# A decoder trunk on one core: turning the gate tokens of the recurrent layer by transposing transfers

## The chip, the core and the metric

The kernel runs on one core of a Trainium2 chip. The metric is the device time of one execution in microseconds; comparisons are made between medians of several runs. The profile is of one execution. Engines: TensorE (PE, with its weight loads as PEld), VectorE (DVE), ScalarE (ACT), GpSimd (POOL) and SyncE (SP), which issues nearly all transfers.

## The reference

256 tokens of width 1024 pass through two layers. Each layer is a SwiGLU FFN, a token mixer and a second FFN, with norms around each. The mixer of the first layer is the recurrent block that the change touches; that of the second is attention over a shared K/V.

```python
def recurrent_block(x, w_in, conv_w, conv_b, w_a, b_a, w_x, b_x, lam, w_out):
    gx = x @ w_in                                    # 1024 -> 2 x 1344
    gate, rec = gx[..., :D_RNN], gx[..., D_RNN:]
    rec = causal_depthwise_conv(rec, conv_w, conv_b) # 4 taps
    rec = rg_lru(rec, w_a, b_a, w_x, b_x, lam)       # two block-diagonal gates, then a scan over time
    return (jax.nn.gelu(gate) * rec) @ w_out         # 1344 -> 1024
```

In `rg_lru` the gates r and i are sigmoids, a = exp(-8 r softplus(-lam)), the scan's input is sqrt(1 - a^2) * i * x. All in float32.

## The kernel before

**Arithmetic.** Every float32 product is made of three matmuls of a rounded upper part and the rest: each weight unit (a 512 KB load, `raw`) is split into `whi` (a copy on ACT, L173) and `wlo` (a subtraction on DVE, L177). There are 5 buffers of `raw` and 9 of each part, so loads and splits run ahead of PE. The tokens are two halves of 128 (t = 0, 1).

**The recurrent stage.** The gate half of `w_in` is computed token-major (tokens in the partitions): column groups g = 0, 1, 2 of `GCOLS`, in units `g0` to `g10`. The recurrent half is computed channel-major (channels in the partitions), since convolution and scan run over time: 11 tiles of 126 channels (the last has 84), two to a pair p = 0 to 5, in units `r0a` to `r5a` (`r4b` is the second half of pair 4's weights). `conv` evacuates a pair to `xc` (ACT) and adds three taps from PSUM (DVE); `gw_unit` makes the two gates (PE, into the two `gt` banks), ACT takes their tanh to `th`. `after_gates` makes tanh and exp on ACT and a few DVE steps. When two pairs are through, `batch(g)` is queued for the four tiles of group g: `roots` (Sqrt on ACT over `tt`, and a Gelu on every gate tile collected in `plain`), `u_of`, `scan`, then the gate tokens are turned to channel-major by PE (`gate_T`, into a `tr` bank), and `product` multiplies them with the scan. Its result is split into an upper part (ACT) and a lower one (`low`, DVE), in `yy[g]`, and `row_items` multiplies these with `w_out` (units w0 to w10, one for each tile of 126 channels k).

**The gate tokens.** When a group is complete, its columns are copied from PSUM to a tile of all 1344 columns for its token half:

```python
tok = toks[t][:, c0:c0 + nn]
if (g, t) == (0, 0):
    nc.scalar.activation(tok, ps, AF.Gelu_apprx_tanh)
else:
    nc.scalar.activation(tok, ps, AF.Copy)
    plain.append(tok)
```

Gelu is therefore done in token order, ahead of the turn. On ACT Gelu, exp (with tanh) and Sqrt each need a table of their own; where the function changes, an `ACT_TABLE_LOAD` stands in its list.

**What sets the order.** PE's order is written by hand: `RG_ORDER` (a unit with its token half in front, as `1g7`) and `OUT_ORDER`, which takes the output rows as eight of half 0 (k = 0 to 7), six of half 1, the last three of half 0, the last five of half 1. After each step `tick` counts down deferred work (`defer(n, fn)`) and takes from `queue` as much as a purse allows. The instructions of the other engines come out of these calls and are then put in order by a scheduler by its own estimates, except those in `keep_in_program_order`. Each engine's list is fixed when the program is built and runs in order: an instruction that waits holds all behind it.

**A turn by transfers, as the FFNs have it.** In the FFNs the hidden activations are turned without PE: POOL separates the 16-bit halves of each float32 into two planes (L515), SP issues a transposing transfer of 16-bit elements (L523), POOL joins the halves again (L528).

Of the kernel before, what the change touches and what calls it, by code (L numbers as in the profile page):

```python
# [43 lines left out]
def trunk_kernel(ctx: ExitStack, tc: tile.TileContext, A: dict, out: bass.AP):  # L44
# [13 lines left out]
    def nm(s):  # L58
        uid[0] += 1
        return f"{s}_{uid[0]}"  # L60
# [146 lines left out]
    def new_ss():  # L207
        return spool.tile([P, 2], F32, tag="ss", name=nm("ss"))

# [432 lines left out]
    GCOLS = [(0, 512), (512, 512), (1024, DRNN - 1024)]  # L642
# [6 lines left out]
    toks = {}  # L649
    plain = []  # L650
    xcs, tt, th, yy = {}, {}, {}, {}

    def add_gate_unit(g, k0, kn):
        c0, nn = GCOLS[g]

        def prep():
            return split(load_raw(w_in(c0, nn, k0, kn), P, kn * nn), P, kn * nn)

        def work(t, u):
            if k0 == 0:  # L660
                gacc[(g, t)] = mmbank()
            ps = gacc[(g, t)][:, :nn]
            for j in range(kn):
                k = k0 + j
                mm3(ps, *main_x(t, k), u.hi[:, j * nn:(j + 1) * nn], u.lo[:, j * nn:(j + 1) * nn], k == 0, k == 7)
            if k0 + kn == 8:

                if t not in toks:
                    toks[t] = pools["r"].tile([P, DRNN], F32, name=f"tok{t}")
                tok = toks[t][:, c0:c0 + nn]  # L670
                if (g, t) == (0, 0):
                    nc.scalar.activation(tok, ps, AF.Gelu_apprx_tanh)
                else:
                    nc.scalar.activation(tok, ps, AF.Copy)
                    plain.append(tok)
        rg[f"g{sum(n[0] == 'g' and n[1] != 'w' for n in rg)}"] = len(items)
        items.append((prep, work))

# [138 lines left out]
    def batch(g):  # L817

        pairs = [p for p in (2 * g, 2 * g + 1)]
        tps, ys = {}, {}  # L820

        def roots():
# [3 lines left out]
            while plain:  # L826
                v = plain.pop(0)
                tc.keep_in_program_order(nc.scalar.activation(v, v, AF.Gelu_apprx_tanh))
# [12 lines left out]
        def gate_T(t):  # L841
            tok = toks[t][:, 4 * g * RT:]
            tp = tps[t] = trbank()
            for j in range(len(pairs) * 2 if g < 2 else 3):
                w = width(4 * g + j)
                nc.tensor.transpose(tp[:w, j * P:(j + 1) * P], tok[:, j * RT:j * RT + w], ident)

        def product(t):
# [4 lines left out]
            for (a, b, w) in parts_of(g):  # L853
                tp = tps[t][:w, a * P:b * P].rearrange("p (a b) -> p a b", a=b - a)
                nc.vector.tensor_tensor(y[:w, a:b, :], tp, tt[g][:w, a:b, t * P:(t + 1) * P], ALU.mult)
# [13 lines left out]
        q.append((0.0, key, lambda: (gate_T(0), gate_T(1))))  # L869
# [591 lines left out]
```

## Time and profile before

| | us |
|---|---|
| median of 3 runs | 968.38 (968.07 to 968.71) |
| the profiled execution, its own time | 968.35 |
| its span in the profile | 966.60 |
| span: PE busy | 958.6 |
| span: DVE busy | 640.1 |
| span: ACT busy | 526.1 |
| span: POOL busy | 193.4 |
| recurrent stage (units g0 to the last output row) | about 189.5 to 300.5 |

The busy shares tell which engine is full on average. A view by stretches gives the same for any piece of the span, with the granted TensorE clock (1.00 throughout) and the share of the transfer engines. The timeline gives start, duration and, in brackets, the idle time ahead of an instruction and what ended it. Matmuls are pipelined, so their durations overlap: their cost is the distance of their starts.

### The profile page before, as it was taken

What the parts mean: (1) busy time and instruction counts of PE and PEld (TensorE: products, weight loads), DVE (VectorE), ACT (ScalarE), POOL (GpSimd) and SP (SyncE); (2) the same over time, 40 slices, a digit from 0 to 9 for tenths busy, and PEclk for the clock granted to TensorE, in tenths of its full rate; (3) what the DMA queues carried; (4) which work ended last, traced back from release to release, by engine and by line L of the source; (5) the groups of instructions that cost most, each with busy time, mean ns of one, the idle gap of its engine ahead of it and who ended that gap; (6) DMA issues with size and microseconds to landing.
All of it is one profiled execution on the core that took longest, in us unless ns stands there. A gap on an engine that the chain in (4) does not pass through costs nothing.

```text
span 966.6 us, 13061 instructions
## 1 busy us (share of the span) xinstructions
PE 958.6 (99%) x4687; PEld 798.1 (83%) x4687; DVE 640.1 (66%) x849; ACT 526.1 (54%) x749; POOL 193.4 (20%) x206
## 2 busy tenths in 40 slices
PE   9999999999999999999999999999999999999997
PEld 6888888898888888888899888888887788888885
DVE  6758764668997666664687466665487876666642
ACT  7446543568886554444555345444366855444431
POOL 2722230100001323230112122224120012232200
PEclk9999999999999999999999999999999999999999
DMA  8778986565346787785589679878762468777731
GB/s 286 224 245 235 270 276 194 159 196 161 113 118 224 215 233 206 207 244 192 131 174 325 179 216 260 226 189 288 230 252 77 132 198 236 207 222 236 217 109 44
DMA packets 142646, 196.83 MB, mean 204 GB/s; under 512 B 58798, under 2 KB 81686, under 8 KB 142454
## 3 DMA queue, kind: packets, MB, share of 16 engines
q1 hardware_dynamic: 139782, 188.96, 66.4%
q0 software_dynamic: 2192, 6.51, 2.6%
q8 instruction: 37, 0.61, 0.3%
q10 hardware_dynamic: 608, 0.53, 0.2%
q14 instruction: 27, 0.22, 0.1%
HBM read 182.32 MB, written 3.16 MB: 192 GB/s over the span
## 4 chain that ended last, share of the span: by engine, by line
PE 96%; DVE 1%; issue 1%; ACT 1%; POOLq 0%; POOL 0%; DVEq 0%; ACTq 0%
PE mm L416 16%; PE mm L417 15%; PE mm L420 15%; PE mm L183 13%; PE mm L185 13%; PE mm L184 13%; PE mm L1027 2%; PE gt L767 2%; PE mm L1296 1%; PE mm L190 1%; PE mm L191 1%; PE mm L192 1%; PE gt L214 1%; PE tr L127 0%; ACT pe L1172 0%
## 5 line engine op out<-in xcount | busy, mean ns | idle before, releaser
L177 DVE TENSOR_TENSOR wlo<-raw,whi 128x1024 fp32r<-128x1024 f32 (+5 forms) x329 | 416.4, 1272 | 226.1 <-ACT whi L173 224.8
L173 ACT ACTIVATE whi<-raw 128x1024 fp32r<-128x1024 f32 (+5 forms) x329 | 341.6, 1045 | 315.5 <-PE mm L420 113.2
L416 PE MATMUL mm<-whi,xhi 128*128 128x512 f32 x656 | 256.7, 391 | 0.0
L417 PE MATMUL mm<-wlo,xhi 128*128 128x512 f32 x656 | 255.5, 390 | 0.0
L420 PE MATMUL mm<-whi,xlo 128*128 128x512 f32 x656 | 202.2, 389 | 0.0
L420 PEld LDWEIGHTS mm<-whi,xlo 128*128 128x128 f32 x656 | 123.1, 188 | 26.0 <-DVE xlo L228 0.2
L416 PEld LDWEIGHTS mm<-whi,xhi 128*128 128x128 f32 x656 | 123.2, 188 | 25.7 <-issue 0.7
L417 PEld LDWEIGHTS mm<-wlo,xhi 128*128 128x128 f32 x656 | 123.2, 188 | 25.1 <-DVE wlo L177 0.3
L183 PE MATMUL mm<-whi,hhi 128*128 128x512 f32 x352 | 137.2, 390 | 0.0
L185 PE MATMUL mm<-whi,hlo 128*128 128x512 f32 x352 | 137.0, 389 | 0.0
L184 PE MATMUL mm<-wlo,hhi 128*128 128x512 f32 x352 | 136.9, 389 | 0.0
L528 POOL COPY pl<-prod 128x1024 uint16<-128x1024 uint16 (+1 forms) x48 | 69.6, 1449 | 173.3 <-DMA prod<-pl 173.3
L515 POOL COPY pl<-prod 128x1024 uint16<-128x1024 uint16 (+1 forms) x48 | 64.1, 1335 | 175.8 <-DVE prod L512 107.0
L184 PEld LDWEIGHTS mm<-wlo,hhi 128*128 128x128 f32 x352 | 66.1, 188 | 13.7
L185 PEld LDWEIGHTS mm<-whi,hlo 128*128 128x128 f32 x352 | 66.1, 188 | 13.7
L183 PEld LDWEIGHTS mm<-whi,hhi 128*128 128x128 f32 x352 | 66.1, 188 | 13.5
L198 POOL TENSOR_SCALAR nv<-ss 128x1 f32<-128x1 f32 x22 | 9.6, 438 | 314.1 <-ACT junk L205 314.1
L512 DVE SCALAR_TENSOR_TENSOR prod<-mm,rstd,sil 128x512 f32<-128x512 f32 (+1 forms) x48 | 33.7, 703 | 28.8 <-PE mm L420 23.1
L503 ACT ACTIVATE sil<-mm,rstd 128x512 f32<-128x512 f32 (+1 forms) x48 | 31.1, 650 | 32.9 <-PE mm L420 25.0
L534 DVE TENSOR_TENSOR hlo<-pl,hhi 128x512 fp32r<-128x512 f32 (+1 forms) x48 | 40.1, 835 | 5.1 <-ACT hhi L533 5.1
L183 PE MATMUL mm<-whi,xhi 128*128 128x512 f32 (+1 forms) x112 | 42.8, 382 | 0.0
L185 PE MATMUL mm<-whi,xlo 128*128 128x512 f32 (+1 forms) x112 | 42.5, 379 | 0.0
(217 smaller groups left out, 1075.1 us busy)
## 6 DMA issues: line engine op xcount, KB each, us to landing
raw<-in_ffn_w_down_dram SPq DMA_DIRECT2D x88, 512.0 KB
raw<-in_ffn_w_up_dram SPq DMA_DIRECT2D x80, 512.0 KB
raw<-in_ffn_w_gate_dram SPq DMA_DIRECT2D x78, 512.0 KB
raw<-in_rg_w_in_dram SPq DMA_DIRECT2D x10, 504.0 KB
raw<-in_rg_w_out_dram SPq DMA_DIRECT2D x10, 504.0 KB
raw<-in_ffn_w_gate_dram SPq DMA_DIRECT2D x19, 256.0 KB
raw<-in_ffn_w_up_dram SPq DMA_DIRECT2D x16, 256.0 KB
raw<-in_rg_w_in_dram SPq DMA_DIRECT2D x8, 512.0 KB
```

The costliest lines, as they stand in the source:

```text
L173: up = nc.scalar.activation(hi[:parts, c:c + m], rawv[:, c:c + m], AF.Copy)
L177: nc.vector.tensor_tensor(lo[:parts, c:c + m], rawv[:, c:c + m], hi[:parts, c:c + m].bitcast(F32), ALU.subtract)
L183: nc.tensor.matmul(ps, xh, wh, start=first, stop=False)
L184: nc.tensor.matmul(ps, xh, wl, start=False, stop=False)
L185: nc.tensor.matmul(ps, xl, wh, start=False, stop=last)
L416: nc.tensor.matmul(ps, get_x(t, k)[0], u.hi[:, c], start=k == 0, stop=False)
L417: nc.tensor.matmul(ps, get_x(t, k)[0], u.lo[:, c], start=False, stop=False)
L420: nc.tensor.matmul(ps, get_x(t, k)[1], u.hi[:, c], start=False, stop=k == nk - 1)
L512: nc.vector.scalar_tensor_tensor(pr[:, :nn], ps, rs[t][:, 0:1], s, ALU.mult, ALU.mult)
L515: nc.gpsimd.tensor_copy(halves.rearrange("p (h f) -> p h f", h=2), pr[:, :nn].bitcast(U16).rearrange("p (f h) -> p h f", h=2))
L528: nc.gpsimd.tensor_copy(halves.rearrange("p (f h) -> p h f", h=2), turned.rearrange("p (h a) b -> p h (a b)", h=2))
L534: keep(nc.vector.tensor_tensor(lv, x, hv.bitcast(F32), ALU.subtract))
```

## The change

The column groups become 504, 504 and 336 wide, which is 4, 4 and 2 tiles of 126 and the one of 84, so a group's columns are those of one `batch`. A unit's weights keep a distance of 512 in their buffers where two k are loaded; `split3` splits them through strided views. Each group's tokens get a tile of their own (`tok`, 512 wide, two buffers). `gate_T` is now called when a group is complete: POOL clears the padding and separates the tokens into planes in which each tile of 126 (or 84) columns takes 128, SP issues one transposing transfer back into `tok`, POOL joins the halves to `tokT` (channels in the partitions, tokens along the free axis). The PE transposes and their `tr` banks go. Gelu is done behind the turn, on `tokT`, by a step `gelu` in the queue of `batch`, in program order; `roots` does only Sqrt. `product` reads `tokT` from SBUF instead of PSUM.

```diff
--- before.py
+++ after.py
@@ -206,6 +206,18 @@
 
     def new_ss():
         return spool.tile([P, 2], F32, tag="ss", name=nm("ss"))
+
+    def planes(dst, src):
+
+        nc.gpsimd.tensor_copy(dst.rearrange("p (h f) -> p h f", h=2), src.bitcast(U16).rearrange("p (f h) -> p h f", h=2))
+
+    def swap(turned, halves):
+
+        tc.keep_in_program_order(nc.sync.dma_start(turned.rearrange("p (a b) -> p a b", b=P), halves, transpose=True))
+
+    def join(dst, turned):
+
+        nc.gpsimd.tensor_copy(dst, turned.rearrange("p (h f) -> p h f", h=2))
 
     def to_tp(src, n):
 
@@ -639,42 +651,71 @@
     n_ffn1 = len(items)
 
 
-    GCOLS = [(0, 512), (512, 512), (1024, DRNN - 1024)]
+    GCOLS = [(0, 504), (504, 504), (1008, DRNN - 1008)]
     rg = {}
 
     def w_in(c0, n, k0, kn):
         return A["rg_w_in"][0, k0 * P:(k0 + kn) * P, c0:c0 + n].rearrange("(k p) n -> p k n", p=P)
 
     gacc = {}
-    toks = {}
-    plain = []
+    tokT = {}
     xcs, tt, th, yy = {}, {}, {}, {}
 
     def add_gate_unit(g, k0, kn):
         c0, nn = GCOLS[g]
 
+        step = 1024 // kn // 64 * 64 if kn < 3 else nn
+
         def prep():
-            return split(load_raw(w_in(c0, nn, k0, kn), P, kn * nn), P, kn * nn)
+            raw = new_raw()
+            v = raw[:, :kn * step].rearrange("p (k n) -> p k n", k=kn)
+            nc.sync.dma_start(v[:, :, :nn], w_in(c0, nn, k0, kn))
+            return split3(raw, kn, step, nn)
 
         def work(t, u):
             if k0 == 0:
                 gacc[(g, t)] = mmbank()
             ps = gacc[(g, t)][:, :nn]
             for j in range(kn):
-                k = k0 + j
-                mm3(ps, *main_x(t, k), u.hi[:, j * nn:(j + 1) * nn], u.lo[:, j * nn:(j + 1) * nn], k == 0, k == 7)
+                k, o = k0 + j, j * step
+                mm3(ps, *main_x(t, k), u.hi[:, o:o + nn], u.lo[:, o:o + nn], k == 0, k == 7)
             if k0 + kn == 8:
-
-                if t not in toks:
-                    toks[t] = pools["r"].tile([P, DRNN], F32, name=f"tok{t}")
-                tok = toks[t][:, c0:c0 + nn]
-                if (g, t) == (0, 0):
-                    nc.scalar.activation(tok, ps, AF.Gelu_apprx_tanh)
-                else:
-                    nc.scalar.activation(tok, ps, AF.Copy)
-                    plain.append(tok)
+                tok = pools["r"].tile([P, 512], F32, tag="tok", name=nm("tok"), bufs=2)
+                nc.scalar.activation(tok[:, :nn], ps, AF.Copy)
+                defer(5 if (g, t) == (0, 0) else 0, lambda: gate_T(g, t, tok, nn))
         rg[f"g{sum(n[0] == 'g' and n[1] != 'w' for n in rg)}"] = len(items)
         items.append((prep, work))
+
+    def split3(raw, kn, step, nn):
+
+        if step == nn:
+            return split(raw[:, :kn * nn], P, kn * nn)
+        u = Unit()
+        hi = wpool.tile([P, 1024], F32R, tag="whi", name=nm("whi"), bufs=WB)
+        lo = wpool.tile([P, 1024], F32R, tag="wlo", name=nm("wlo"), bufs=WB)
+        v, hv, lv = (x[:, :kn * step].rearrange("p (k n) -> p k n", k=kn)[:, :, :nn] for x in (raw, hi, lo))
+        nc.scalar.activation(hv, v, AF.Copy)
+        nc.vector.tensor_tensor(lv, v, hv.bitcast(F32), ALU.subtract)
+        u.hi, u.lo = hi, lo
+        return u
+
+    def gate_T(g, t, tok, nn):
+
+        m = 4 if g < 2 else 3
+        halves = hpool.tile([P, 512], F32, tag="t1", name=nm("pl"), bufs=2).bitcast(U16)[:, :2 * m * P]
+        hv = halves.rearrange("p (h j f) -> p h j f", h=2, j=m)
+        src = tok[:, :nn].bitcast(U16)
+        n = nn // RT
+        nc.gpsimd.memset(hv[:, :, :n, RT:], 0)
+        nc.gpsimd.tensor_copy(hv[:, :, :n, :RT], src[:, :2 * n * RT].rearrange("p (j f h) -> p h j f", h=2, f=RT))
+        if n < m:
+            nc.gpsimd.memset(hv[:, :, n, BLK:], 0)
+            nc.gpsimd.tensor_copy(hv[:, :, n, :BLK], src[:, 2 * n * RT:].rearrange("p (f h) -> p h f", h=2))
+        turned = tok.bitcast(U16)[:, :2 * m * P]
+        out = tokT[g, t] = pools["r"].tile([P, 4, P], F32, tag="tokT", name=nm("tokT"), bufs=6)
+        defer(1, lambda: swap(turned, halves))
+        defer(5, lambda: join(out[:, :m, :].rearrange("p a b -> p (a b)").bitcast(U16).rearrange(
+            "p (f h) -> p h f", h=2), turned))
 
     def tiles_of(p):
         return [2 * p, 2 * p + 1] if p < 5 else [10]
@@ -817,15 +858,12 @@
     def batch(g):
 
         pairs = [p for p in (2 * g, 2 * g + 1)]
-        tps, ys = {}, {}
+        ys = {}
 
         def roots():
             for (a, b, w) in parts_of(g):
                 v = tt[g][:w, a:b, :]
                 nc.scalar.activation(v, v, AF.Sqrt)
-            while plain:
-                v = plain.pop(0)
-                tc.keep_in_program_order(nc.scalar.activation(v, v, AF.Gelu_apprx_tanh))
 
         def u_of(p):
             w, m = pw(p), len(tiles_of(p))
@@ -838,12 +876,11 @@
             v = tt[g][:w, 2 * (p % 2) + j, :]
             nc.vector.tensor_tensor_scan(v, th[p][0][:w, j, :], v, 0.0, ALU.mult, ALU.add)
 
-        def gate_T(t):
-            tok = toks[t][:, 4 * g * RT:]
-            tp = tps[t] = trbank()
-            for j in range(len(pairs) * 2 if g < 2 else 3):
-                w = width(4 * g + j)
-                nc.tensor.transpose(tp[:w, j * P:(j + 1) * P], tok[:, j * RT:j * RT + w], ident)
+        def gelu():
+            for t in range(2):
+                for (a, b, w) in parts_of(g):
+                    v = tokT[g, t][:w, a:b, :]
+                    tc.keep_in_program_order(nc.scalar.activation(v, v, AF.Gelu_apprx_tanh))
 
         def product(t):
             y = ys[t] = pools["r"].tile([RT, 4, P], F32, tag="y", name=nm("y"), bufs=2)
@@ -851,8 +888,7 @@
                 yy[g] = [rw.tile([P, 1024], F32R, tag="gy", name=nm("y"), bufs=6).rearrange("p (t a b) -> p t a b", t=2, a=4)
                          for _ in range(2)]
             for (a, b, w) in parts_of(g):
-                tp = tps[t][:w, a * P:b * P].rearrange("p (a b) -> p a b", a=b - a)
-                nc.vector.tensor_tensor(y[:w, a:b, :], tp, tt[g][:w, a:b, t * P:(t + 1) * P], ALU.mult)
+                nc.vector.tensor_tensor(y[:w, a:b, :], tokT[g, t][:w, a:b, :], tt[g][:w, a:b, t * P:(t + 1) * P], ALU.mult)
                 nc.scalar.activation(yy[g][0][:w, t, a:b, :], y[:w, a:b, :], AF.Copy)
 
         def low(t):
@@ -866,7 +902,7 @@
             s = len(tiles_of(p)) / 2
             q.append((1.3 * s, key, lambda p=p: u_of(p)))
             q += [(0.72, key, lambda p=p, j=j: scan(p, j)) for j in range(len(tiles_of(p)))]
-        q.append((0.0, key, lambda: (gate_T(0), gate_T(1))))
+        q.insert(-1, (0.0, key, gelu))
         for t in range(2):
             q.append((0.7, key, lambda t=t: product(t)))
         for t in range(2):
```

In the order of ACT's list, from pair 2's `xc` to the Sqrt of group 0 (`tt`); before:

```order
L720 ACTIVATE xc_2133<-mm_2084,par 126x256 x2
L781 ACTIVATE th_2152<-gt_2139,hb 126x256
L781 ACTIVATE th_2153<-gt_2139,hb 126x256
L781 ACTIVATE th_2152<-gt_2140,hb 126x256
L781 ACTIVATE th_2153<-gt_2140,hb 126x256
L800 ACTIVATE tt_2061<-th_2152,sp_101 126x256 x2
L800 ACTIVATE th_2152<-th_2152,sp_102 126x256 x2
L173 ACTIVATE whi_2335<-raw_2333 128x1008
L173 ACTIVATE whi_2384<-raw_2382 128x672
L825 ACT_TABLE_LOAD
L825 ACTIVATE tt_2061<-tt_2061 126x1024
```

Now:

```order
L761 ACTIVATE xc_2151<-mm_2102,par 126x256 x2
L883 ACT_TABLE_LOAD
L883 ACTIVATE tokT_1893<-tokT_1893 126x512
L822 ACTIVATE th_2171<-gt_2158,hb 126x256
L822 ACTIVATE th_2171<-gt_2159,hb 126x256
L822 ACTIVATE th_2172<-gt_2158,hb 126x256
L822 ACTIVATE th_2172<-gt_2159,hb 126x256
L841 ACTIVATE tt_2078<-th_2171,sp_101 126x256 x2
L841 ACT_TABLE_LOAD
L841 ACTIVATE th_2171<-th_2171,sp_102 126x256 x2
L883 ACT_TABLE_LOAD
L883 ACTIVATE tokT_2071<-tokT_2071 126x512
```

Two Gelu on `tokT`, each with its table load, and a reload of the table of exp stand ahead of the Sqrt (which follows the last row here, with a load of its own); the two splits `whi_2335` and `whi_2384` (r4b and r5a) have gone behind it.

DVE's list around the first reader of that Sqrt. `wlo_2336` and `wlo_2385` before, `wlo_2368` and `wlo_2409` now are the lower splits of r4b and r5a; before:

```order
L805 TENSOR_SCALAR th_2152<-th_2152 126x512
L806 SCALAR_TENSOR_TENSOR th_2153<-tt_2061,th_2152 126x512
L177 TENSOR_TENSOR wlo_2336<-raw_2333,whi_2335 128x1008
L809 SCALAR_TENSOR_TENSOR th_2153<-th_2153,th_2152 126x512
L177 TENSOR_TENSOR wlo_2385<-raw_2382,whi_2384 128x672
L810 TENSOR_SCALAR th_2152<-th_2153 126x512
L833 SCALAR_TENSOR_TENSOR tt_2061<-th_2042,tt_2061 126x512
L833 SCALAR_TENSOR_TENSOR tt_2061<-th_2153,tt_2061 126x512
L834 TENSOR_TENSOR tt_2061<-tt_2061,xc_1952 126x512
L834 TENSOR_TENSOR tt_2061<-tt_2061,xc_2022 126x512
```

Now, from eight rows behind the reader on:

```order
L767 SCALAR_TENSOR_TENSOR xc_2263<-mm_2210,par,xc_2263 126x255
L872 TENSOR_TENSOR tt_2078<-tt_2078,xc_2035 126x512
L767 SCALAR_TENSOR_TENSOR xc_2263<-mm_2210,par,xc_2263 126x254
L877 SCALAR_TENSOR_TENSOR tt_2078<-th_2171,tt_2078 126x256
L767 SCALAR_TENSOR_TENSOR xc_2263<-mm_2210,par,xc_2263 126x253
L877 SCALAR_TENSOR_TENSOR tt_2078<-th_2171,tt_2078 126x256
L177 TENSOR_TENSOR wlo_2368<-raw_2365,whi_2367 128x1008
L891 TENSOR_TENSOR y_2371<-tokT_1893,tt_2078 126x512
L891 TENSOR_TENSOR y_2390<-tokT_2071,tt_2078 126x512
L177 TENSOR_TENSOR wlo_2409<-raw_2406,whi_2408 128x672
L897 TENSOR_TENSOR y_2373<-y_2371,y_2372 126x512
L177 TENSOR_TENSOR wlo_2430<-raw_2427,whi_2429 126x1024
```

The two lower splits stood ahead of L833 (L871 now); they now stand among the products and the low parts of group 0. The reader, L871 on `tt_2078`, stands eight rows above the first row here.

SP's list, with the loads of `w_in`'s last unit and of w0 to w4:

```order
L161 DMA raw_2365<-in_rg_w_in_dram 128x4x252
L216 DMA_TRANSPOSE tok_2066<-pl_2068 128x8x128
L161 DMA raw_2406<-in_rg_w_in_dram 128x8x84
L164 DMA raw_2427<-in_rg_w_out_dram 126x1024
L164 DMA raw_2455<-in_rg_w_out_dram 126x1024
L164 DMA raw_2511<-in_rg_w_out_dram 126x1024
L216 DMA_TRANSPOSE tok_2294<-pl_2296 128x8x128
L164 DMA raw_2532<-in_rg_w_out_dram 126x1024
L216 DMA_TRANSPOSE tok_2348<-pl_2350 128x6x128
L164 DMA raw_2586<-in_rg_w_out_dram 126x1024
```

The three transposing transfers, of (0, 1), (1, 1) and (2, 0), are new; the loads around them stand in the same sequence as before, and none stood between them.

## The prediction

> **What bounds the kernel now.** I read the busy shares and the chain that ended last first, then the stretches of the recurrent stage one by one.
>
> ```profile
> PE 958.6 (99%) x4687; PEld 798.1 (83%) x4687; DVE 640.1 (66%) x849; ACT 526.1 (54%) x749; POOL 193.4 (20%) x206
> PE 96%; DVE 1%; issue 1%; ACT 1%; POOLq 0%; POOL 0%; DVEq 0%; ACTq 0%
> 220.00:240.00 20.00, 20.00 (x138) 18.08 (x138) 16.94 (x30) 18.37 (x29) 0.00 (x0) 1.00 0.59 165
> 240.00:260.00 20.00, 20.00 (x144) 17.99 (x143) 19.53 (x34) 17.61 (x33) 0.00 (x0) 1.00 0.45 142
> 260.00:280.00 20.00, 19.54 (x102) 16.22 (x102) 19.06 (x36) 19.88 (x32) 0.00 (x0) 1.00 0.21 60
> 238.78:288.46 49.68, 49.22 (x293) 42.44 (x293) 48.27 (x84) 44.51 (x72) 0.00 (x0) 1.00 0.40 121
> ```
>
> The last four rows are stretches: limits, length, then busy time of PE, PEld, DVE, ACT and POOL. Over the kernel PE is the bound, and any TensorE instruction taken off is time. In the second half of the recurrent stage two more engines are as full: DVE is busy 48.27 of 49.68 us, ACT 19.88 of 20. Whether DVE is on the path is seen at the last output rows:
>
> ```profile
> L185 PEld LDWEIGHTS mm<-whi,y 126*128 126x128 f32 x40 | 7.5, 188 | 1.7 <-DVE y L861 0.2
> 288.75 0.39 PE L184 MATMUL mm<-wlo,y 126*128 126x512 f32 x1
> 288.98 0.44 PE L185 MATMUL mm<-whi,y 126*128 126x512 f32 x1
> 288.46 0.61 DVE L861 TENSOR_TENSOR y<-y,y 126x256 fp32r<-126x256 f32 x2
> ```
>
> PE reaches the first row of group 2 (k = 8, token half 0) just as DVE has written the low part of its product: the weight load of `y` waits 0.2 us for L861, and the matmul at 288.98 is a little long (0.44 instead of 0.39). PE and DVE arrive together. So the saving on PE counts only if DVE's list also gets shorter by then, and every microsecond by which it gets longer counts in full.
>
> **What is removed.** The PE transposes of the gate tokens, in the chain of waits:
>
> ```profile
> 247.69 0.87 PE tr L846 x8
> 266.49 0.87 PE tr L846 x8
> 267.37 0.46 issue
> 281.18 0.66 PE tr L846 x6
> ```
>
> 0.87 + 0.87 + 0.66 = 2.40 us, and the 0.46 us gap behind the second (PE waits there for a PSUM bank that ACT reads) could go too: at most 2.86. The new widths are neutral. Matmuls of 512 columns start 0.23 us apart (288.75 and 288.98 above), those of 320 columns 0.15:
>
> ```profile
> 244.30 0.31 PE L185 MATMUL mm<-whi,xlo 128*128 128x320 f32 x1
> 244.45 0.31 PE L183 MATMUL mm<-whi,xhi 128*128 128x320 f32 x1
> ```
>
> Both are about 0.45 ns a column, and the columns stay the same: 96 matmuls lose 8 each, 48 gain 16 each. Sum 0.
>
> **ACT, ahead of the square root of group 0.** Before, ACT took the tanh and exp of pair 1, two weight splits (r4b, r5a), then Sqrt. Now it also loads the Gelu table and does one Gelu ahead of those tanh, reloads the exp table, and loads Gelu's again for a second Gelu; the two splits go behind the Sqrt.
>
> ```profile
> 229.30 1.00 ACT L720 ACTIVATE xc<-mm,par 126x256 f32<-126x256 f32 x2
> 231.25 1.57 ACT L781 ACTIVATE th<-gt,hb 126x256 f32<-126x256 f32 x4 [0.95 <-PE gt L767]
> 233.69 1.10 ACT L800 ACTIVATE th<-th,sp 126x256 f32<-126x256 f32 x2
> 234.67 1.71 ACT L173 ACTIVATE whi<-raw 128x1008 fp32r<-128x1008 f32 x2
> 236.39 1.28 ACT L825 ACT_TABLE_LOAD   x1
> 237.69 1.06 ACT L825 ACTIVATE tt<-tt 126x1024 f32<-126x1024 f32 x1
> 240.06 1.15 ACT L828 ACTIVATE tok<-tok 128x512 f32<-128x512 f32 x2
> ```
>
> From these starts: load 1.30, Gelu 0.55, tanh with the step behind them 2.44 (231.25 to 233.69), exp 0.98. From 230.30, when `xc` is done: 230.30 + 1.30 + 0.55 + 2.44 + 1.30 + 0.98 + 1.30 + 0.55 + 1.30 = 240.02 for the start of Sqrt, where it was 237.69. PE has those gates ready at 231.25, so of the first load and Gelu 0.95 us lies in a gap. Sqrt comes **2.3 us later** and ends at 241.08. (The Gelu on the very first copy and its table load go; ACT waits for PE right behind them, so 0.)
>
> **DVE, which waits for that Sqrt.**
>
> ```profile
> 235.89 1.20 DVE L177 TENSOR_TENSOR wlo<-raw,whi 128x1008 fp32r<-128x1008 f32 x1
> 237.00 0.69 DVE L809 SCALAR_TENSOR_TENSOR th<-th,th 126x512 f32<-126x512 f32 x1
> 237.61 0.85 DVE L177 TENSOR_TENSOR wlo<-raw,whi 128x672 fp32r<-128x672 f32 x1
> 238.38 0.42 DVE L810 TENSOR_SCALAR th<-th 126x512 f32<-126x512 f32 x1
> 238.78 1.29 DVE L833 SCALAR_TENSOR_TENSOR tt<-th,tt 126x512 f32<-126x512 f32 x2
> ```
>
> L833 at 238.78 is the first reader of Sqrt. Before, DVE filled the wait with the lower splits of r4b and r5a (235.89 to 237.00 and 237.61 to 238.38, 1.88 us). Now these stand behind the scans of group 0, so DVE waits with nothing to do until 241.08 and then has them on top. From there to the low part of group 2 its list is the same as before: 48.27 us of work, so 241.08 + 48.27 + 1.88 = 291.23 instead of 288.46, if the old 1.41 us of gaps (49.68 - 48.27) close; with them 292.6. **Term A: +2.77 us**, up to 4.18. The product now reads two SBUF operands instead of PSUM and SBUF; same size, I take 0. PE's 2.86 us are swallowed: it only comes earlier to the same wait.
>
> **POOL, which did nothing here.** Its copies lock DVE out:
>
> ```profile
> 75.33 1.90 POOL L515 COPY pl<-prod 128x1024 uint16<-128x1024 uint16 x1 [7.50 <-ACT hhi L533]
> 75.11 1.22 DVE L177 TENSOR_TENSOR wlo<-raw,whi 128x1024 fp32r<-128x1024 f32 x1
> 76.24 1.53 DVE L534 TENSOR_TENSOR hlo<-pl,hhi 128x512 fp32r<-128x512 f32 x1
> 65.61 0.68 DVE L534 TENSOR_TENSOR hlo<-pl,hhi 128x512 fp32r<-128x512 f32 x1
> L534 DVE TENSOR_TENSOR hlo<-pl,hhi 128x512 fp32r<-128x512 f32 x40 | 36.7, 918 | 2.6 <-ACT hhi L533 2.6
> L177 DVE TENSOR_TENSOR wlo<-raw,whi 128x1024 fp32r<-128x1024 f32 x292 | 376.7, 1297 | 217.6 <-ACT whi L173 216.5 <-DMA raw<-in_ffn_w_up_dram 0.4
> 62.20 1.04 POOL L515 COPY pl<-prod 128x1024 uint16<-128x1024 uint16 x1 [3.84 <-DVE prod L512]
> 66.48 1.34 POOL L528 COPY pl<-prod 128x1024 uint16<-128x1024 uint16 x1 [3.24 <-DMA prod<-pl]
> 131.12 0.61 POOL L515 COPY pl<-prod 128x512 uint16<-128x512 uint16 x1
> 134.36 0.78 POOL L528 COPY pl<-prod 128x512 uint16<-128x512 uint16 x1 [2.63 <-DMA prod<-pl]
> ```
>
> The POOL copy that starts at 75.33 sits out DVE's 75.11 instruction (1.90 instead of 1.04), and then DVE's next one sits out the copy (1.53 instead of 0.68, +0.85). Averaged over the FFNs' 96 copies the loss is smaller: 292 x (1.297 - 1.22) + 40 x (0.918 - 0.68) = 32 us, 0.33 each, since DVE has gaps there. Behind 241 us there are eight copies: two planes and a join for each of the last three tiles, less one. By size: 1.02 + 2 x (0.61 + 0.32) + 1.34 + 2 x 1.06 = 6.34 us (0.32 and 1.06 drawn between the rows). Bounds for DVE: 8 x 0.33 = 2.6 and 6.3. DVE is 97% busy here, which speaks for the row at 76.24, but the convolution taps read PSUM, and L512, which does too, shows no such loss. I take the middle, **term B: +4.5 us**. The Trainium skill, "SBUF — State Buffer", section "SBUF: two separate sides", says that a DVE instruction with two SBUF inputs and a GpSimd one that reads SBUF hold one port pair for a whole instruction and the loser blocks; the trace agrees at 76.24. By that rule the product, now with two SBUF inputs, joins those that can be blocked, and the sum would go to the upper bound, 977.5. The copies and joins of the first three tiles meet DVE ahead of its wait for Sqrt and cost 0.
>
> **New waits in the queues.** A transpose on SP waits for POOL's planes copy, with weight loads behind it:
>
> ```profile
> 63.27 1.25 SPq L523 DMA_TRANSPOSE prod<-pl  x1
> 237.12 1.69 SPq L164 DMA_DIRECT2D raw<-in_rg_w_out_dram  x2
> ```
>
> From planes done (63.24) to join (66.48) is 3.24 us, all in 6 to 7. The fourth transpose waits for tokens that ACT copies behind Sqrt, `xc`, two splits, a load and four tanh: 241.08 + 1.00 + 1.71 + 1.30 + 1.57 = 246.7. With 0.6 for that copy, 1.02 for the planes and 1.25 for the issue, w3's load goes out at about 249.6 instead of 237.12. PE wants w3 some 5 us behind the gap at 267.37 (three rows of six matmuls at 0.23 us, 4.1, and the gates): 20 us of cover. ACT comes to its split at about 253.6, behind the product of group 0 (15 DVE instructions from 241.08, some 9 us), two y copies, an exp and two splits: 4 us for the load to land, against 3.24 for the transfer above. I take 0; without that cover ACT would stand in front of `xc` of pair 4. The Gelu waits on ACT are for joins done 5 us or more earlier: 0.
>
> **Sum.** The profiled execution took 968.35 us (span 966.60 plus 1.75); the median of the runs is 968.38. 968.35 + 2.77 + 4.5 = **975.6**. After the stage the program is the same and PE-bound, so nothing is given back. Its own range: 968.35 + 2.77 = 971.1 without any lock, 968.35 + 4.18 + 6.34 = 978.9 with all.
>
> **Rivals.**
> - *Faster (0.14):* the low part of group 2 is not what PE waits for, because the scheduler's shuffle lets DVE come to it no later than before; then PE's saving is plain: 968.35 - 2.86 = 965.5. For it: the wait at L861 is 0.2 us in one place and PE is busy 99%. Against: DVE's list is in order, 97% full, and starts 2.3 us late. It decides if low(t0) of group 2 ends before 288.5.
> - *No change (0.10):* POOL's copies fall on taps and scans, and ACT is up to 1.5 us quicker than my walk: 968.4 to 970.3.
> - *SP stops ACT (0.07):* w3 or w4 lands 3 us later than I think, ACT stands in front of `xc` of pair 4, the taps and gates of pair 4 follow: 975.6 + 3 = 978.6.
> - *A table switch costs twice what its row shows (0.03):* each of the three loads added ahead of Sqrt empties the engine for as long again, 3 x 1.30 = 3.9 more: 979.5. Against: between 236.39 and 237.69 there is room for the load alone. The Trainium skill states such a rule, "ScalarE: Activation LUTs", section "What ACT_TABLE_LOAD costs": some 1380 ns of drain beside 1283 ns of load; by it the estimate would be 3 x 1.38 = 4.1 more.
> - That the transposes stay on PE is out: they are gone from its list.
>
> **Chances.** My forecast has 0.66. Within 0.2% (1.94 us, about what a measurement of this kernel can tell from no change) is the second rival, 0.10; faster the first, 0.14; slower the rest, 0.66 + 0.07 + 0.03 = 0.76. The range leaves out the faster rival and the far end: 966.4 to 979.5.
>
> **What would show it.** Right: no `tr` rows of tokens on PE; Sqrt of group 0 near 240 and an idle gap of about 2 us on DVE before its L871 (the new L833); PE idle between 248 and 292 us, at the gate matmuls of pair 4, at the first row of group 1, and most at the first of group 2, released by DVE; DVE instructions of 512 elements above 1 us beside POOL copies; from 300 us on the same pattern, shifted. Wrong in A: Sqrt before 238.5, or DVE with gaps between 241 and 290. Wrong in B: the mean of L177's 126x1024 splits still at 1.22 us. Wrong altogether: PE without idle time in the stage, and a span about 2.4 us shorter.

## The result, and the profile after

The changed kernel takes 974.54 us (median of 6 runs, 974.38 to 976.42) against 968.44 us before: ratio 1.0067, 95% interval 1.0056 to 1.0078. It is 6.1 us slower; 975.6 was forecast. Its profiled execution has a span of 974.1 us and took 975.82 us, which is above the median. Part of that lies ahead of the stage: the first gate matmul (the reader's mark for the stage's start, in the timeline of TensorE, first before, then after) comes 0.60 us later although nothing there has changed; the first transposes of the input, near the program's start, are already 0.61 us later (8.79 instead of 8.18 us). Times within the stage are compared from this mark below.

```profile
216.90 2.95 PE L767 MATMUL gt<-xc,gw 126*126 126x256 f32 x16
```
```profile
217.50 2.74 PE L808 MATMUL gt<-xc,gw 126*126 126x256 f32 x14
```

The stretches of the stage after the change (limits, length, busy time of PE, PEld, DVE, ACT and POOL, then clock, DMA share and GB/s), and TensorE's waits from 222 to 302 us:

```profile
220.00:240.00 20.00, 20.00 (x141) 17.83 (x138) 15.77 (x26) 18.88 (x30) 3.35 (x4) 1.00 0.59 158
260.00:280.00 20.00, 16.46 (x77) 12.40 (x75) 20.00 (x35) 17.99 (x31) 6.32 (x1) 0.91 0.41 121
242.02:295.47 53.45, 47.82 (x257) 39.18 (x256) 53.33 (x84) 45.73 (x75) 19.30 (x10) 0.97 0.46 124
```
```profile
PE gt L808 <- ACT th L841: 2.2, 1, 2.2
PE mm L185 <- DVE y L897: 1.8, 1, 1.8
PE gt L808 <- ACT whi L173: 1.3, 1, 1.3
PE mm L192 <- DVE wlo L177: 0.6, 1, 0.6
```

Between 220 and 240 us DVE has lost work (15.77 us busy instead of 16.94). From its first reader of Sqrt (242.02) to the low part of group 2 (295.47) it is busy for 53.33 of 53.45 us; before, the same piece of its list took 48.27 of 49.68. TensorE, which lost 0.46 us there before, now waits 5.9 us at four places: 3.5 at the gates of pair 4, 1.8 at the first row of group 2, for DVE, and 0.6 for the lower split of r4b, one of the two that moved behind Sqrt. The timeline of ACT shows why DVE starts late:

```profile
230.91 1.28 ACT L883 ACT_TABLE_LOAD   x1
232.21 0.63 ACT L883 ACTIVATE tokT<-tokT 126x512 f32<-126x512 f32 x1
234.17 1.10 ACT L841 ACTIVATE tt<-th,sp 126x256 f32<-126x256 f32 x2
235.29 1.28 ACT L841 ACT_TABLE_LOAD   x1
236.58 1.09 ACT L841 ACTIVATE th<-th,sp 126x256 f32<-126x256 f32 x2
237.69 1.28 ACT L883 ACT_TABLE_LOAD   x1
239.64 1.28 ACT L866 ACT_TABLE_LOAD   x1
240.94 1.06 ACT L866 ACTIVATE tt<-tt 126x1024 f32<-126x1024 f32 x1
```

Four table loads, each right behind the instruction ahead of it, stand where one stood, and Sqrt starts at 240.94 instead of 237.69. DVE's and POOL's timelines behind it (a bracket at the end of a row is the idle time before it):

```profile
242.02 1.29 DVE L871 SCALAR_TENSOR_TENSOR tt<-th,tt 126x512 f32<-126x512 f32 x2 [1.97 <-ACT tt L866]
253.12 1.79 DVE L897 TENSOR_TENSOR y<-y,y 126x512 fp32r<-126x512 f32 x1
255.97 0.68 DVE L897 TENSOR_TENSOR y<-y,y 126x512 fp32r<-126x512 f32 x1
256.58 1.48 DVE L842 SCALAR_TENSOR_TENSOR xc<-th,xc 126x512 f32<-126x512 f32 x1
265.21 0.67 DVE L842 SCALAR_TENSOR_TENSOR xc<-th,xc 126x512 f32<-126x512 f32 x1
288.87 1.15 DVE L871 SCALAR_TENSOR_TENSOR tt<-th,tt 84x256 f32<-84x256 f32 x1
295.47 0.61 DVE L897 TENSOR_TENSOR y<-y,y 126x256 fp32r<-126x256 f32 x2
```
```profile
252.63 1.81 POOL L220 COPY tokT<-tok 128x1024 uint16<-128x1024 uint16 x1
256.47 1.10 POOL L220 COPY tokT<-tok 128x768 uint16<-128x768 uint16 x1 [1.91 <-DMA tok<-pl]
273.68 10.81 POOL L710 COPY pl<-tok 128x504 uint16<-128x504 uint16 x1 [16.11 <-ACT tok L684]
287.75 2.04 POOL L220 COPY tokT<-tok 128x768 uint16<-128x768 uint16 x1 [2.80 <-DMA tok<-pl]
```

The low part at 253.12 takes 1.79 us beside a join, its sister at 255.97 takes 0.68; L842 at 256.58 takes 1.48 beside the next join, at 265.21 without one 0.67. These are the lock's marks. The copy at 273.68 shows the other side of it: 10.81 us for 504 columns, most of it waiting, as the short copies below show.

### The profile page after: what moved, and what is told of

It reads as the page before. It is cut to its first block, busy times and chain, and to the rows that moved or that the text cites. A ratio compares the mean times of both kernels' runs of the same rounds, so it can differ in the third digit from the quotient of the medians.

```text
span 974.1 us, 13059 instructions
## 1 busy us (share of the span) xinstructions
PE 959.1 (98%) x4665; PEld 796.4 (82%) x4665; DVE 644.9 (66%) x849; ACT 530.1 (54%) x754; POOL 226.4 (23%) x228
## 4 chain that ended last, share of the span: by engine, by line
PE 87%; DVE 4%; ACT 3%; DMA 2%; issue 2%; POOL 1%; POOLq 0%; ACTq 0%; DVEq 0%
PE mm L428 15%; PE mm L429 15%; PE mm L432 15%; PE mm L183 11%; PE mm L185 11%; PE mm L184 11%; PE mm L1063 2%; DVE wlo L177 1%; POOL pl L710 1%; PE mm L1332 1%; DMA raw<-in_w_kv_dram 1%; PE gt L808 1%; PE gt L226 1%; ACT whi L173 1%; PE mm L190 1%
## 5 line engine op out<-in xcount | busy, mean ns | idle before, releaser
L177 DVE TENSOR_TENSOR wlo<-raw,whi 128x1024 fp32r<-128x1024 f32 (+4 forms) x320 | 405.4, 1272 | 229.2 <-ACT whi L173 227.6
L173 ACT ACTIVATE whi<-raw 128x1024 fp32r<-128x1024 f32 (+4 forms) x320 | 333.8, 1047 | 321.3 <-PE mm L432 122.4
L540 POOL COPY pl<-prod 128x1024 uint16<-128x1024 uint16 (+1 forms) x48 | 72.2, 1504 | 169.6 <-DMA prod<-pl 169.6
L527 POOL COPY pl<-prod 128x1024 uint16<-128x1024 uint16 (+1 forms) x48 | 66.2, 1380 | 175.9 <-DVE prod L524 106.4
L183 PE MATMUL mm<-whi,xhi 128*128 128x512 f32 (+2 forms) x112 | 42.9, 383 | 0.0
L185 PE MATMUL mm<-whi,xlo 128*128 128x512 f32 (+2 forms) x112 | 42.5, 380 | 0.0
```

The costliest lines, as they stand in the source:

```text
L173: up = nc.scalar.activation(hi[:parts, c:c + m], rawv[:, c:c + m], AF.Copy)
L177: nc.vector.tensor_tensor(lo[:parts, c:c + m], rawv[:, c:c + m], hi[:parts, c:c + m].bitcast(F32), ALU.subtract)
L183: nc.tensor.matmul(ps, xh, wh, start=first, stop=False)
L185: nc.tensor.matmul(ps, xl, wh, start=False, stop=last)
L527: nc.gpsimd.tensor_copy(halves.rearrange("p (h f) -> p h f", h=2), pr[:, :nn].bitcast(U16).rearrange("p (f h) -> p h f", h=2))
L540: nc.gpsimd.tensor_copy(halves.rearrange("p (f h) -> p h f", h=2), turned.rearrange("p (h a) b -> p h (a b)", h=2))
```

## The experiments

In the edits, `...` and the comments stand for code that is left out. Two theories stood against each other. **Theory 1**, the prediction's: DVE's list sets the end, late behind Sqrt (A) and lengthened by POOL's locks (B). **Theory 2**: the transfers' own chain sets it (the starved POOL copy, the weight loads on SP behind it, ScalarE in front of a missing weight). The changed kernel's chain that ended last, followed back from the end, speaks for theory 2; it runs through the starved copy, its join, group 2's Gelu and ScalarE's splits to the low part:

```profile
273.68 10.81 POOL pl L710
287.75 2.05 POOL tokT L220
295.47 0.43 DVE y L897
```

That view names at each step what came last. DVE's 53.33 busy us of 53.45 speak for theory 1: a list in order without gaps cannot end earlier because something else does. "Start" below is DVE's first reader of Sqrt counted from the first gate matmul, "list" the time from there to the low part of group 2.

**Group 0's Gelu behind its Sqrt.**

```diff
+            if g == 0:
+                gelu()              # at the end of roots()
-        q.insert(-1, (0.0, key, gelu))
+        if g > 0:
+            q.insert(-1, (0.0, key, gelu))
```

> Group 0's two Gelu go back behind its Sqrt (as before the change), which also brings the weight splits of r4b and r5a back ahead of that Sqrt; the transposing transfers and all POOL copies stay. Theory 1 (VectorE's list sets the end: it starts late behind Sqrt and is lengthened by POOL's locks): VectorE's first L871 (here two or three lines lower) comes about 2.6 us earlier in the stage, 2.15 us of splits leave the list behind it, up to 1.4 us of old gaps come back: 3.4 to 4.8 us less than the changed kernel, 970 to 971 us. Theory 2 (the transfers' chain sets the end: POOL's 10.8 us copy, SP's late loads, Gelu of group 2): that chain is not touched, within 1 us of the changed kernel, 973.5 to 975.5 us.

Measured: 971.17 us, ratio 1.0030 (1.0018 to 1.0042), 3.4 us less than the changed kernel, at the edge of what theory 1 said and far from theory 2. Theory 2's chain did not stay quite untouched, though: the copy of 504 columns takes 3.92 us here instead of 10.81. In its timeline Sqrt starts at 239.28, with the stage's mark at 218.50. DVE's list, its first and its last row and the stretch between them:

```profile
241.42 1.28 DVE L873 SCALAR_TENSOR_TENSOR tt<-th,tt 126x512 f32<-126x512 f32 x2
292.78 0.61 DVE L899 TENSOR_TENSOR y<-y,y 126x256 fp32r<-126x256 f32 x2
```
```profile
241.42:292.78 51.36, 48.90 (x264) 40.45 (x263) 50.98 (x84) 46.18 (x76) 15.38 (x10) 0.97 0.44 126
```

With A gone and all transfers in place, 2.86 us remain over the kernel before: B by itself. From the mark they show at two places. The list is 1.68 us longer (51.36 instead of 49.68), and its start is 22.92 us instead of 21.88, though Sqrt stands where it stood (20.78 instead of 20.79): beside an early join, at 228.24, a DVE instruction at 229.16 takes 1.79 us instead of 0.69. The changed kernel has the same lock, but there DVE waits 1.97 us for Sqrt afterwards, which hides it.

**POOL's copies cut to one or eight columns.**

```diff
-        nc.gpsimd.tensor_copy(hv[:, :, :n, :RT], ...)
+        nc.gpsimd.tensor_copy(hv[:, :1, :min(n, 3), :1], ...)
-        defer(5, lambda: join(...))
+        defer(5, lambda: nc.gpsimd.tensor_copy(...[:, :, :8], ...[:, :, :8]))
```

> The POOL copies in front of and behind the transposing transfers move one or eight columns instead of all (the gating tokens are left out of the result); every other instruction, wait and transfer stays in its place. Theory 1: the 3.8 us that VectorE's instructions lose beside these copies go, the late Sqrt stays: 970 to 971.5 us. Theory 2: the 10.8 us copy and the waits behind it go as well, and SP's loads come 1 to 2 us earlier; if these set the end, up to 6 us go, 968.5 us. A theory in which POOL does not touch VectorE and only the late Sqrt counts: 974 us, unchanged.

Measured: 981.01 us, ratio 1.0127 (1.0114 to 1.0141). Neither theory said so. A part of it is the edit's own: the copies write to fixed tiles that are filled with zeros ahead of the stage, and the mark stands at 218.40, 1.50 us late. POOL's, ScalarE's and DVE's timelines of this kernel:

```profile
252.32 7.09 POOL L726 COPY ft<-tok 128x16 uint16<-128x16 uint16 x1 [3.18 <-DMA tok<-ft]
280.36 10.24 POOL L719 COPY ft<-tok 128x2 uint16<-128x2 uint16 x1 [17.56 <-ACT tok L693]
```
```profile
265.70 1.06 ACT L173 ACTIVATE whi<-raw 126x1024 fp32r<-126x1024 f32 x1 [8.31 <-DMA raw<-in_rg_w_out_dram]
```
```profile
258.65 0.68 DVE L857 SCALAR_TENSOR_TENSOR th<-tt,th 126x512 f32<-126x512 f32 x1
267.70 0.48 DVE L777 SCALAR_TENSOR_TENSOR xc<-mm,par,xc 126x255 f32<-126x255 f32 x1 [8.37 <-ACT xc L771]
```

A copy of 16 columns lasts 7.09 us and one of two columns 10.24 us: the length does not come from the size. The first ends at 259.41, just when DVE runs out of work (258.65 + 0.68 = 259.33). Behind it on POOL stands a planes copy, behind that on SP a transfer and behind that a weight load; ScalarE waits 8.31 us for it and DVE 8.37 for ScalarE. So theory 2's chain exists and can decide: here it does.

**The same with SP freed.** 
```diff
-        nc.gpsimd.tensor_copy(hv[:, :1, :min(n, 3), :1], ...)
+        if g + t < 2:                   # else: the transfer reads a tile of zeros
+            nc.gpsimd.tensor_copy(hv[:, :1, :min(n, 3), :1], ...)
```

> The run with POOL copies of one or eight columns came out at 981.0 us, where its expectation was 970 to 971.5; its trace names the planes copy behind a join that waited 7.1 us for VectorE, and behind that SP with w4's load. Here the planes copies of the last three tiles are left out, so that their transposing transfers read a tile of zeros and wait for ScalarE's copy alone; the joins of eight columns stay, and the filling of the tiles with zeros no longer stands ahead of the norms' POOL steps (1.3 us there). If the starved POOL copy in front of SP was the cause: the 8.3 us of ScalarE's wait for the load go, 972 to 973 us, like the run with the three tiles left out. If the short copies are slow for another reason: 978 us and more.

Measured: 973.93 us (972.45 to 974.75), up to 1 us above what was expected and 7 us below the run before, of which 1.27 lie ahead of the stage (mark at 217.13). The profiled execution is the fastest, 972.45. The 8.3 us wait is gone (two waits of 1.36 and 1.03 us are left), and starved copies stay (the POOL row holds two copies, of which the first takes 7.43 us):

```profile
250.70 7.55 POOL L726 COPY ft<-tok 128x16 uint16<-128x16 uint16 x2 [24.47 <-DMA tok<-fx]
```
```profile
241.65:292.76 51.11, 48.06 (x256) 40.33 (x256) 49.45 (x85) 46.20 (x75) 13.03 (x3) 0.93 0.49 129
```

DVE loses nothing to locks here (49.45 us busy, as in the run below that leaves the last three tiles out), while transfers and starved joins are in place. The two runs differ by 1.6 us in the median (973.93 and 972.37) and by less than 0.1 in their profiled executions (972.45 and 972.37): beside A, transfers and starved joins cost something between nothing and 1.6 us.

**w3's load ahead of the fourth transfer on SP.**

```diff
-        defer(1, lambda: swap(turned, halves))
+        defer(5 if (g, t) == (1, 1) else 1, lambda: swap(turned, halves))
-        defer(5, lambda: join(...))
+        defer(8 if (g, t) == (1, 1) else 5, lambda: join(...))
```

> The transposing transfer of the fourth token tile is issued behind the load of output row block w3 instead of ahead of it, so that this load no longer waits for ScalarE's copy and POOL's planes copy. Theory 1: ScalarE's 2.5 us of waits for that load and TensorE's 3.5 us at the gates of pair 4 shrink, but VectorE, which never idles from 242 us on, is as late as it was: 974.0 to 975.0 us, unchanged. Theory 2 (SP's late loads, by way of ScalarE and the gates, set the end): 2 to 3.5 us less, 971 to 972.5 us.

Measured: 974.57 us (1.0055 to 1.0081), the changed kernel's 974.54. The list is as long as ever (241.31 to 294.50, 53.19 us). But the edit does not free the load: it goes out 33.24 us behind the mark, in the changed kernel 33.22 (250.72). In both it waits for its raw buffer, which the moved split of r4b frees (in the changed kernel at 249.52 + 1.18 = 250.70), and not for the transfer. So theory 2 is not tested by this run in the way that was meant. What it shows is that TensorE's waits at the gates can grow, from 3.5 to 5.8 us in all, and the time stays as it was: in the changed kernel they lie under DVE's lateness.

**The last three tiles left out, A kept.**

```diff
+        if (g, t) in tokT:              # (1, 1), (2, 0), (2, 1): tiles of zeros
+            return                      # at the head of gate_T
```

> The last three token tiles (of groups 1 and 2) are left out: no POOL copies, no transposing transfers and no joins for them, their Gelu reads zeros; the first three and ScalarE's order stay, so the late Sqrt stays. Theory 1 (late Sqrt plus POOL's locks on VectorE): the locks behind 241 us, 3.8 us, go: 970.7 us (970 to 971.5). Theory 3 (POOL's copies do not lengthen VectorE's list; the late Sqrt is all): 974 us. The short copies of the second run could not tell this, because there a copy of 16 columns waited 7.1 us for VectorE and held SP's loads back.

Measured: 972.37 us, ratio 1.0046 (1.0033 to 1.0058): 2.2 us less than the changed kernel, not 3.8; 4.07 us over the kernel before. The mark, the list's stretch (columns as above) and two rows of DVE's and ScalarE's timelines have the reason:

```profile
216.76 2.96 PE L814 MATMUL gt<-xc,gw 126*126 126x256 f32 x16
```
```profile
241.29:292.39 51.10, 48.09 (x256) 40.40 (x256) 49.45 (x85) 46.19 (x75) 0.00 (x0) 0.93 0.39 116
```
```profile
259.27 0.48 DVE L773 SCALAR_TENSOR_TENSOR xc<-mm,par,xc 126x255 f32<-126x255 f32 x1 [1.58 <-ACT xc L767]
```
```profile
255.66 1.06 ACT L173 ACTIVATE whi<-raw 126x1024 fp32r<-126x1024 f32 x1 [1.82 <-DMA raw<-in_rg_w_out_dram]
```

DVE's busy time falls by 53.33 - 49.45 = 3.88 us, what the locks had taken, but 1.58 us of a wait come up that they had covered: ScalarE has no weight for its split, because the loads wait for raw buffers, and those are freed by DVE's splits, which start late: the two loads that went out from 237.12 on, behind the splits of r4b and r5a, now go out at 249.60 and 251.57, with no transfer ahead of them. So A costs more than its late start. The edit takes away both the locks and theory 2's chain, so it does not by itself tell which of the two the 2.2 us belong to; DVE's full list says the locks.

**A and short copies both away.** The first and the second edit together.

> Both of the first two edits: group 0's Gelu behind Sqrt, and POOL's copies of one or eight columns (gating tokens left out of the result). Theory 1: the two savings add, 3.4 to 4.8 and 3.8 us off 974.5, 966 to 967.5 us, at or a little below the kernel before, and TensorE's saved transposes (2.4 to 2.9 us) set the floor at 965.5 us. Theory 2: little more than the shorter copies alone.

Measured: 968.85 us, ratio 1.0004 (0.9995 to 1.0013), 1 to 2 us above what was expected. Its mark stands 1.99 us late:

```profile
218.89 2.96 PE L818 MATMUL gt<-xc,gw 126*126 126x256 f32 x16
```

Only 0.35 of that is there at the first transposes of the input; the other 1.64, as many as in the run with short copies alone, go with the tiles that are filled with zeros ahead of the norms' POOL steps, where TensorE waits 1.3 us (in the run with SP freed, where the fills come later, the mark is at 217.13). Within the stage start and list are 21.88 and 48.80 us (before: 21.88 and 49.68): both terms are gone. From the mark the low part of group 2 comes at 70.68 us, 0.88 earlier than before, and the end of the span 1.09 earlier. So in the time the kernel before is reached; within the stage it is beaten by about a microsecond, a part of what TensorE saves.

**POOL copies added to the kernel before**, read by nobody.

```diff
+        nc.gpsimd.tensor_copy(a, tok[:, :n].bitcast(U16)...)      # planes, into scratch
+        defer(5, lambda: nc.gpsimd.tensor_copy(scratch[1]..., a)) # join, into scratch
```

> The kernel before with POOL copies of the sizes of the planes and joins added for all token tiles but the last, into scratch that nobody reads: four of them fall behind 241 us, nothing waits for them, all other engines' lists are those of before. Theory 1: VectorE loses 0.33 to 1 us to each of the four: 969.6 to 972 us, half of what the changed kernel loses for its eight (1.3 to 2 us) being likeliest, 969.6 to 970.3. Theory 3: 968.3 us, no change.

Measured: 968.61 us (0.9996 to 1.0014): +0.3 us, a miss. Its list, 238.61 to 289.16, is 50.55 us, 0.87 longer than before. DVE is busy for 50.17 of it, 1.90 more than the 48.27 before: just under half a microsecond for each of the four copies, which ran between 245.9 and 252.3 us. A lock takes as much as in the changed kernel, but here most of it goes into gaps that DVE's list had anyhow (1.41 us before, 0.38 now).

**Three tiles by transfer, three on TensorE**, all Gelu behind the square roots.

```diff
+                by_pe = g + t > 1
+                if by_pe:
+                    plain.append(tok[:, :nn])       # Gelu in roots(), then L846's transposes
+                else:
                     defer(5 if (g, t) == (0, 0) else 0, lambda: gate_T(g, t, tok, nn))
```

> The first three token tiles by transfers (their POOL copies come ahead of 230 us), the last three by TensorE's transposes as before, all Gelu behind the square roots as before: 1.3 us of transposes are saved, without a new order on ScalarE and without copies behind 241 us. Theory 1 (TensorE comes earlier to the same wait for VectorE's low part): 967.9 to 968.5 us, like before. Theory 4 (TensorE alone sets the time once A and B are gone): 967.0 us.

Measured: 968.33 us, ratio 1.0001 (0.9992 to 1.0010): theory 1. 1.3 us of transposes less on TensorE are worth nothing in the time, and the early lock's late start (22.90 us) does no harm either, as the list is 1.2 us shorter than before (48.51). It computes the whole reference and is as good as the kernel before, not better.

**Where TensorE's saving went.** Four kernels relieve DVE or ScalarE further, to see it appear: two lower splits less for DVE (first piece), Gelu for group 0 alone for ScalarE (second piece), or both. But for the one built on the kernel before, they leave out the last three tiles and have group 0's Gelu behind its Sqrt; the early lock is in them, with a start of 22.9 us.

```diff
+                if len(widths) == NRT and k in (3, 5):   # w_out rows 3 and 5: no lower split
+                    ...
+                    u.hi = u.lo = hi
```
```diff
-            for t in range(2):
+            for t in range(2 if g == 0 else 0):     # in gelu()
```

> As the run with the last three tiles left out, with group 0's Gelu behind Sqrt, and VectorE's list shortened by two weight splits of w_out (rows 3 and 5 use the upper part twice, 2.4 us of VectorE, no change on TensorE). Theory 1: VectorE no longer comes last at group 2, and the saved transposes show: 965.5 to 966.0 us, 2.4 to 2.9 us below the kernel before. If another engine (ScalarE is as full) takes VectorE's place: 967 to 968.5 us.

Measured: 968.75 us (0.9993 to 1.0011). DVE now stands idle for ScalarE, and the low part is no earlier:

```profile
273.35 0.43 DVE L859 TENSOR_SCALAR th<-th 126x512 f32<-126x512 f32 x1 [1.79 <-ACT th L854]
288.52 0.61 DVE L912 TENSOR_TENSOR y<-y,y 126x256 fp32r<-126x256 f32 x2
```

> The kernel before with the same two weight splits less on VectorE, nothing else. TensorE comes to the first row of group 2 just with VectorE (0.2 us of wait), and keeps its transposes, so VectorE's 2.4 us are worth 0.2 to 0.5 us: 967.8 to 968.3 us. If VectorE alone set the end before the change: 965.9 us.

Measured: 969.14 us (0.9999 to 1.0018): not even 0.2 us are gained. The same idle time stands in the same place (1.72 us at 273.94).

> The last three tiles left out and group 0's Gelu behind Sqrt, as in the run before; VectorE's splits are all there again, but ScalarE is relieved: the Gelu of groups 1 and 2 are left out with three table loads (some 6.5 us of ScalarE). If VectorE's list alone holds group 2: 968 to 968.8 us, as with VectorE relieved alone. If ScalarE alone held it: 965.5 to 966 us.

Measured: 967.61 us (0.9985 to 1.0002), 0.9 below the kernel before, which the interval does not tell from no change.

> Both relieved: as the run above, and two weight splits less on VectorE (2.4 us). If the two engines hold the time together and TensorE is next: TensorE's saved transposes show now, 965.5 to 966.2 us. If a fourth wait (weight loads, PSUM banks) stands behind them: 967 us and more, and its name is in the waits of TensorE.

Measured: 967.14 us, ratio 0.9988 (0.9979 to 0.9997), 1.4 below. ScalarE's relief gives most of it; what DVE's adds, 0.5 us, the intervals do not tell from nothing. Behind the two TensorE has a wait at the gates, which no engine's row explains:

```profile
PE gt L821 <- issue: 1.2, 1, 1.2
```

Half of TensorE's 2.86 us came out in the time, and only with 6.5 us of ScalarE and 2.4 of DVE left out. Where the rest stays is open. About a microsecond came out within the stage in the run with A and short copies both away, which has neither the early lock nor anything less on ScalarE or in DVE's splits.

## Why the prediction was right, point by point

- **Direction and sum: right.** DVE's low part of group 2 sets the end; from the mark it is 6.41 us later (77.97 instead of 71.56), the median 6.1. 7.27 was the sum of A and B.
- **A, start: right.** Sqrt 240.94, less the 0.60 us of the mark 240.34, against 240.02; DVE idle for 1.97 us before L871; start 24.52 instead of 21.88 us, +2.64 for the 2.3.
- **A, list: mis-sized.** "If the old 1.41 us of gaps close" was the weak step. They close only under the locks. Alone, A costs 2.65 us of start and 1.42 of list (51.10 - 49.68), 4.07 in all, as the run with three tiles left out took over the kernel before; forecast 2.77, or up to 4.18 with all the old gaps, near what came. What was not foreseen is that the two moved splits also free raw buffers late.
- **B: mechanism right, size too high.** DVE's instructions lose 3.88 us to eight copies (0.49 each, within the bounds of 2.6 and 6.34), but only 2.2 us of time (974.54 - 972.37) hang on what the last three tiles bring, and 2.9 (971.17 - 968.31) on all six where A is away; 4.5 were forecast. That the first three cost 0 holds only as long as DVE waits for Sqrt behind them; without A their lock makes the start 1.04 us late. The Trainium skill, "SBUF — State Buffer", section "SBUF: two separate sides", has such an operation block fully for the other's instruction; the 1.79 and 1.48 us rows agree. The upper sum from it, 977.5, did not come; why a copy takes half a microsecond from DVE and not its whole length is not shown.
- **The sum came close by luck:** A was 1.3 us short and B 2.3 too large, and these offset each other. Alone the two measure 4.07 (95% interval 3.2 to 5.6) and 2.86 (1.7 to 4.1), together 6.1 (5.4 to 7.6), so the intervals do not show whether they add. The traces do show one overlap: of the 2.86, 1.04 are the early lock, which A's wait for Sqrt hides.
- **A sign that was badly chosen:** "wrong in B if the splits' mean is still 1.22". It is, and B is there all the same; the locks fell on other instructions of the list:

```profile
L177 DVE TENSOR_TENSOR wlo<-raw,whi 126x1024 fp32r<-126x1024 f32 x10 | 12.1, 1206 | 0.0
L897 DVE TENSOR_TENSOR y<-y,y 126x512 fp32r<-126x512 f32 x4 | 3.8, 956 | 0.0
L842 DVE SCALAR_TENSOR_TENSOR xc<-th,xc 126x512 f32<-126x512 f32 x3 | 2.8, 943 | 0.0
```

- **TensorE's waits:** at the gates of pair 4 and the first row of group 2, as forecast; none at the first row of group 1, more at the gates (3.5 us) than at group 2 (1.8), and one of 0.6 for a moved split that was not forecast.
- **SP's late loads taken as 0: right for the time, wrong for the trace and the cause.** ScalarE does stand in front of `xc` of pair 4. The load goes out at 250.72, near the 249.6 of the forecast, but by luck: it waits for the buffer of a moved split, not for the transfer, and with no transfer ahead of it it hardly goes out earlier (249.60, which is 32.84 us behind that run's mark, against 33.22). Beside the locks this costs nothing that a run shows; without them it is the 1.58 us of DVE's wait above. The rival was one step away, as the short copies showed.
- **Table switch at twice its row: out.** L841's pair ends at 235.27 and the load starts at 235.29; all four loads follow the instruction ahead of them like this. The 1380 ns of drain in the Trainium skill ("ScalarE: Activation LUTs", "What ACT_TABLE_LOAD costs") is in no gap here.
- **"The new widths are neutral": a small miss.** The rows are the first and the last of a run of 24 matmuls of the third column group, before and after:

```profile
244.01 0.30 PE L183 MATMUL mm<-whi,xhi 128*128 128x320 f32 x1
247.38 0.31 PE L185 MATMUL mm<-whi,xlo 128*128 128x320 f32 x1
```
```profile
244.59 0.32 PE L183 MATMUL mm<-whi,xhi 128*128 128x336 f32 x1
248.13 0.33 PE L185 MATMUL mm<-whi,xlo 128*128 128x336 f32 x1
```

3.37 against 3.54 us for 23 steps, 0.1465 against 0.154 each, or 0.36 us for 48; the groups of 504 start 0.228 us apart, those of 512 0.229, and give next to nothing back.

## What to carry to other kernels

Where two engines come to a row at the same time, work taken off one is worth little: ask first what the other, and the third behind it, does then. A step that is turned over to transfers brings its order with it; here three table loads ahead of one Sqrt, and two splits that moved behind it and freed their buffers late, cost more than the transposes saved. When two costs hide each other's waits, measure each alone and both together before adding them. And look at where an edit took effect: a load that was moved ahead in its queue left no earlier, and a fill ahead of the stage hid a microsecond that was gained in it.

## What the runs showed of the hardware

- POOL can starve beside a full DVE. Copies of 2, 16 and 504 columns took 10.24, 7.09 and 10.81 us, and the one of 16 ended within 0.1 us of DVE's first idle moment. The other seven copies of the changed kernel's last three tiles, beside the same DVE, took 0.5 to 2.0 us; what makes the difference is not shown. A short copy can wait as long as a long one, and whatever waits for it in a queue (here weight loads) is held as long.
- A DVE instruction beside a copy can be longer by about a microsecond (1.79 instead of 0.68, 1.48 instead of 0.67). Eight copies took 3.88 us of DVE in the changed kernel, four in the kernel before 1.90: just under half a microsecond each in both. How much of that is time depends on the gaps in DVE's list: the time grew by 2.2 us in the first and by 0.3, within its interval, in the second.
- In the stretch with the waits at pair 4's gates, 260 to 280 us, TensorE's granted clock was 0.91 (1.00 before). That this cost nothing here, as TensorE was waiting for DVE anyhow, is argued and not measured.
